# Two lengths in a planner's table, set to what the trace shows: transposing transfers and output products

## The chip, the cores and the metric

The kernel runs on one core of a Trainium2 chip. The metric is the device time of one execution in microseconds (us). It is given as the median of three runs; a profile is one further execution, with a time of its own.

## The reference

One hybrid encoder layer is applied to two sequences with the same weights: 1024 rows (prompt) and 4096 rows (sample), each row 1024 wide, all in float32.

```python
h = rms_norm(x, norm_g)
proj = h @ w_in                                   # 1024 -> 2816 columns
q, k, v, g_attn, u_conv, g_conv = split(proj)
attn = windowed_gqa(q, k, v, sink)                # 8 heads x 64, 128-row blocks, keys of 3 blocks
val, gate = split(u_conv)
c = depthwise_conv31(val * sigmoid(gate)) + dw_b  # 512 channels, 31 taps
conv = silu(layer_norm(c, ln_g, ln_b))
mix = concat(attn * silu(g_attn), conv * silu(g_conv))
y = rms_norm(x + mix @ w_out, final_g)
```

## The kernel before, in words

Rows are worked on in groups of 512 (two of the prompt, eight of the sample), and a group in four blocks of 128. Float32 products are made out of halves: a high and a low part, three products for each pair. The program has two stages, each recorded as a list of operations and then put in order by a planner.

**Stage A** (to about 896 us) makes the attention. `prep_x` normalizes a block of rows and splits it into high and low float16 parts (tile `xt`), and `dma_t` moves them, transposed, to the tile `x16` (`x` in the trace). `group_proj` makes keys, values, queries and gates from it with `inproj` (L347: 24 matmuls a tile, 128 weights columns by 512 rows). `attention` does one block: for each of two halves of the heads, four score products (L492, L493) into one of three PSUM tiles `s`; VectorE adds the distance penalty and takes the maximum (L496); ScalarE takes exponentials (L505) and normalizes (L512), VectorE makes the low part (L513), in one of three tiles `pe`; and `dma_t` moves `pe` transposed to a tile `pT`. When both halves have landed, TensorE makes the block's output `o` (L528, 18 matmuls, 12 at the ends of a sequence), VectorE and ScalarE multiply by the gate and split (L535, L536, L537), and the result goes to device memory (`md`). At its end the stage also makes the conv inputs of the first group: four tiles `h` (L638, L639) and four gates (L645), from the same `x16`.

**Stage B** makes the convolution, the output product and the final norm. For each group: load the next group's `x16` back (`x<-xd`), make its `h` tiles and gates (288 matmuls of L347), run 31 taps of the convolution over this group's four channel tiles on VectorE (L701, L703, tiles `acc`), turn `acc` on TensorE (L714) for the layer norm, turn it back (L750), and for each block make the output product from the stored attention part `ma` and the conv part `mc` (`out_mm`, L769, 24 matmuls each), add the residual (L800), and norm it on GpSimd (L803 and the lines 257 to 266, L813) before the store (`y`).

**The order.** `Plan.flush` is a list scheduler that runs when the kernel is built. Each operation is recorded with an engine and a cost in ns. The planner keeps a time for each engine and one for the transfers, picks whichever operation can start first (the earliest recorded one among equals), and emits them in order of planned start. Each engine, and the one queue of SyncE (SP) that issues all transfers, then works strictly in that order on the chip. The planner adds 1000 ns ahead of a transfer, `nbytes / 295` (transposing, `dma_t`) or `nbytes / 360` (plain, `dma`), one after the other, and 1600 ns behind. A transposing transfer of an attention half has 2048 x 384 = 786,432 bytes, of 2048 x 256 at the ends of a sequence; one of `xt` has 524,288. The cost of a pair of output matmuls in `out_mm` is 432 ns. Of VectorE's work the planner counts a tap (`c_dve(512, 1)`) as 663 ns.

```python
if o.eng == "SP":
    self.free["SP"] = s + 60.0
    self.dma = max(self.dma, s + 1000.0) + o.cost
    o.end = self.dma + 1600.0
```

Of the kernel before, what the change touches and what calls it, by code (L numbers as in the profile page):

```python
# [197 lines left out]
def hymba_kernel(ctx, tc, x_p, x_s, w_in, norm_g, sink, dw_w, vecs, w_out, final_g, dist, y_p, y_s):  # L198
    nc = tc.nc
    V, S, T, GP = nc.vector, nc.scalar, nc.tensor, nc.gpsimd  # L200
    PSUM = bass.MemoryType.PSUM
    pl = Plan(tc)
# [23 lines left out]
        pl.op("SP", nbytes / 360.0, lambda: nc.sync.dma_start(dst(), src()), r=r, w=w)  # L226

    def dma_t(dst, src, nbytes, r, w):
        pl.op("SP", nbytes / 295.0, lambda: nc.sync.dma_start(dst(), src(), transpose=True), r=r, w=w)

    ident = cst.tile([P, P], F32, name="ident")
    make_identity(nc, ident)
# [140 lines left out]
    def split_x(x16, b, xb, xt, rs, rv):  # L373
        pl.op("ACT", c_act(1024, 1), lambda: S.activation(xt.t[:, 0], xb.t, AF.Copy, scale=rv()), [xb, rs], [(xt, 0)])
        pl.op("DVE", c_dve(1024, 1), lambda: V.scalar_tensor_tensor(xt.t[:, 1], xb.t, rv(), xt.t[:, 0], ALU.mult, ALU.subtract), [xb, rs, (xt, 0)], [(xt, 1)])
        dma_t(lambda: x16.t[:, :, :, b * P : (b + 1) * P].rearrange("p a k t -> p (a k) t"), lambda: xt.t.rearrange("p a c -> p (a c)"), 524288, [xt], [(x16, b)])
# [88 lines left out]
    def attention(gi, qb, cur, prev):  # L465
# [11 lines left out]
        for kv in range(2):  # L477
            def one(kv=kv):
# [32 lines left out]
                for hh in range(4):  # L511
                    pl.op("ACT", c_act(n, 1), lambda hh=hh: S.activation(p16(hh, 0), sc_(hh), AF.Copy, scale=rc.t[:, hh : hh + 1]), [rc, (pe, hh + 2)], [(pe, hh)])  # L512
                    pl.op("DVE", c_dve(n, 1), lambda hh=hh: V.scalar_tensor_tensor(p16(hh, 1), sc_(hh), rc.t[:, hh : hh + 1], p16(hh, 0), ALU.mult, ALU.subtract), [rc, (pe, hh + 2)], [(pe, hh)])  # L513
                nk = len(kbs)
                dma_t(lambda: pT.t[:, : 8 * nk, :], lambda: flat().bitcast(F16)[:, : 8 * n], 2048 * n, [(pe, hh) for hh in range(4)], [pT])
                pTs.append(pT)
            one()
# [151 lines left out]
    wo = Buf(None, None, pb.tile([P, KD, 2, D], F32R, name="wo"))  # L669
# [94 lines left out]
    def out_mm(po, m, k0):  # L764
        for k in range(k0, k0 + 4):
            for a, b in ((0, 0), (0, 1), (1, 0)):
                def mm(k=k, a=a, b=b):
                    for hf in range(2):
                        T.matmul(  # L769
                            po[hf].t, m.t[:, a, k - k0, :], wo.t[:, k, b, hf * 512 : (hf + 1) * 512],  # L770
                            start=(k == 0 and a == 0 and b == 0), stop=(k == KD - 1 and a == 1),
                        )
                pl.op("PE", 432, mm, [(m, a) if k0 else m, (wo, k)], po)

    def out_first(gi, qb):
        si, g, n_g = groups[gi]
        ab = g * NB + qb
        src = seqs[si][0]
        tail = gi == NG - 1 and qb % 2 == 1
        xb = spare(qb, [P, D], F32) if tail and qb > 0 else pl.buf(pxA, [P, D], F32, "xb", 2)  # L780
        dma(lambda: xb.t, lambda: src[ab * P : (ab + 1) * P, :], 524288, [], [xb])
        ma = spare(0, [P, 2, 4, P], F32R) if tail else pl.buf(pb, [P, 2, 4, P], F32R, "ma", 1)
        md = mscr[si, ab]
        dma(lambda: ma.t.rearrange("p a j t -> p (a j t)").bitcast(F32), lambda: md.t, 524288, [md], [ma])
        po = [pl.buf(psq, [P, 512], F32, "mm", 4) for _ in range(2)]
        out_mm(po, ma, 0)
        return xb, po

    def out_second(gi, qb, xb, po, mc, eng="POOL"):
        en = GP if eng == "POOL" else V  # L790
        si, g, n_g = groups[gi]
        ab = g * NB + qb
        dst = seqs[si][1]
        out_mm(po, mc, 4)
        ms, v, rs = small(smB, 2, "ms2", 2), small(smB, 1, "v2", 2), small(smB, 1, "r2", 2)
        for hf in range(2):
            def half(hf=hf):
                xs = lambda: xb.t[:, hf * 512 : (hf + 1) * 512]
                sq = spare(4, [P, 512], F16) if gi == NG - 1 else po[hf]
                pl.op("DVE", c_dve(512), lambda: V.tensor_tensor(xs(), xs(), po[hf].t, ALU.add), [po[hf], (xb, hf)], [(xb, hf)])  # L800
                pl.op("ACT", c_act(512) + 100, lambda: S.activation(sq.t, xs(), AF.Square, scale=1.0 / math.sqrt(D), accum_out=ms.t[:, hf : hf + 1]), [(xb, hf)], [sq, (ms, hf)])  # L801
            half()
        pl.op(eng, 650 if en is GP else 140, lambda: en.tensor_scalar(v.t, ms.t[:, 0:1], ms.t[:, 1:2], EPS, ALU.add, ALU.add), [ms], [v])  # L803
        rsqrt(smB, rs, v, "o", eng)
        if en is V:
            for hf in range(2):
                def last(c=slice(hf * 512, (hf + 1) * 512), hf=hf):
                    pl.op("DVE", c_dve(512, 1), lambda: V.scalar_tensor_tensor(xb.t[:, c], xb.t[:, c], rs.t, fg.t[:, c], ALU.mult, ALU.mult), [(xb, hf), rs, fg], [(xb, hf)])
                    dma(lambda: dst[ab * P : (ab + 1) * P, c], lambda: xb.t[:, c], 262144, [(xb, hf)], [])
                last()  # L810
            return
        pl.op("ACT", c_act(1024, 1), lambda: S.activation(xb.t, xb.t, AF.Copy, scale=rs.t), [xb, rs], [xb])  # L812
        pl.op("POOL", 2400, lambda: GP.tensor_tensor(xb.t, xb.t, fg.t, ALU.mult), [xb, fg], [xb])  # L813
        dma(lambda: dst[ab * P : (ab + 1) * P, :], lambda: xb.t, 524288, [xb], [])

    curs[0]["gates"] = True
    for gi in range(NG):
# [16 lines left out]
        for b0, nb in chunks:  # L834
# [6 lines left out]
            for i in range(nb):  # L841
                xb, po = out_first(gi, b0 + i)
# [56 lines left out]
```

## Time and profile before

| | |
|---|---|
| median of three runs | 2024.65 us (2024.41 to 2028.73) |
| the profiled execution | 2031.13 us, its span 2029.3 us |
| busy: TensorE / VectorE / ScalarE / GpSimd | 92% / 89% / 45% / 33% of the span |
| mean granted TensorE clock | 0.983 of full speed |

The profile was taken in an execution 6.5 us above the median, and 1.8 us of its time lie outside the span. Times inside the trace are counted from the start of the span.

### The profile page before, as it was taken

The numbers are of one execution on the slowest core, as the hardware profiler recorded it, in microseconds if no ns is written. First come the engines' busy times: TensorE is split into PE (matmuls) and PEld (weight loads), VectorE is DVE, ScalarE is ACT, GpSimd is POOL, SyncE is SP. The second block draws the span as 40 slices with busy tenths as digits, with TensorE's granted clock in tenths as the row PEclk, the third lists the DMA queues.
The fourth block names the chain that finished last, engine by engine and source line by source line (L and its number), as shares of the span: only waits on it lengthen the run. The fifth ranks groups of instructions, "written<-read, shape, count | busy, mean of one in ns | idle before, by whom it ended". The sixth has DMA issues, their size and how long they took to land.

```text
span 2029.3 us, 26112 instructions
## 1 busy us (share of the span) xinstructions
PE 1874.0 (92%) x8953; PEld 1033.5 (51%) x8953; DVE 1809.5 (89%) x3779; ACT 904.5 (45%) x1962; POOL 670.8 (33%) x908
## 2 busy tenths in 40 slices
PE   2999999899999999989999899999999989999997
PEld 1444444444444444434647456474745647475675
DVE  6787988888978887879999899999989999898997
ACT  3576787787787876730303222220312212131332
POOL 3412233233321310000434627063461806143264
PEclk9999999999999999999999999999999999999999
DMA  7575979899989999772212211121221203123031
GB/s 243 148 174 131 241 186 230 192 197 225 223 192 242 221 300 272 149 238 84 94 42 94 83 68 68 52 95 42 94 73 59 89 21 123 42 94 104 25 122 73
DMA packets 367526, 276.18 MB, mean 136 GB/s; under 512 B 328736, under 2 KB 328864, under 8 KB 363808
## 3 DMA queue, kind: packets, MB, share of 16 engines
q1 hardware_dynamic: 367392, 274.51, 50.1%
q8 instruction: 70, 1.15, 0.2%
q14 instruction: 64, 0.52, 0.1%
HBM read 115.09 MB, written 77.59 MB: 95 GB/s over the span
## 4 chain that ended last, share of the span: by engine, by line
DVE 40%; PE 31%; DMA 10%; ACT 9%; POOL 6%; issue 3%; SPq 0%; DVEq 0%; ACTq 0%; POOLq 0%
DVE acc L703 23%; PE mm L347 16%; PE mm L769 10%; DMA pT<-pe 7%; DVE pe L496 3%; ACT pe L512 2%; ACT pe L505 2%; PE o L528 2%; DVE pe L513 2%; POOL rs_oa L264 1%; DVE xb L800 1%; DVE wA L703 1%; POOL xb L813 1%; POOL v L803 1%; DVE h L639 1%
## 5 line engine op out<-in xcount | busy, mean ns | idle before, releaser
L347 PE MATMUL mm<-x,wA 128*128 128x512 f16 x4800 | 1086.0, 382 | 14.7 <-DMA x<-xd 7.8
L703 DVE SCALAR_TENSOR_TENSOR acc<-h,taps,acc 128x512 f32<-128x512 f32 (+2 forms) x1380 | 867.7, 688 | 1.4
L347 PEld LDWEIGHTS <-wA 128*128 128x128 f16 x4800 | 468.5, 98 | 564.0 <-issue 29.5
L769 PE MATMUL mm<-wo,mc 128*128 128x512 f32 x960 | 236.5, 402 | 6.7 <-ACT mc L760 5.3
L769 PE MATMUL mm<-wo,ma 128*128 128x512 f32 x888 | 217.4, 400 | 7.5 <-DMA ma<-md 7.3
L496 DVE CUSTOM_DVE_ANT_0 pe<-s,dist_sb,sink_sb 128x384 f32<-128x384 f32 (+1 forms) x320 | 200.2, 658 | 21.3 <-DMA pT<-pe 11.5
L513 DVE SCALAR_TENSOR_TENSOR pe<-pe,rc 128x384 f16<-128x384 f32 (+1 forms) x320 | 190.2, 629 | 30.5 <-ACT pe L512 29.2
L803 POOL TENSOR_SCALAR v<-ms 128x1 f32<-128x1 f32 x38 | 46.9, 1233 | 509.7 <-ACT mm L801 498.9
L505 ACT ACTIVATE pe<-pe,nm 128x384 f32<-128x384 f32 (+1 forms) x320 | 188.9, 591 | 47.1 <-DVE nm L501 46.4
L769 PEld LDWEIGHTS mm<-wo,mc 128*128 128x128 f32 x960 | 180.3, 190 | 50.0 <-ACT mc L760 6.1
L512 ACT ACTIVATE pe<-pe,rc 128x384 f16<-128x384 f32 (+1 forms) x320 | 176.8, 593 | 37.1 <-DVE rc L509 21.9
L769 PEld LDWEIGHTS mm<-wo,ma 128*128 128x128 f32 x888 | 167.7, 189 | 49.1 <-issue 7.5
L812 ACT ACTIVATE xb<-xb,r 128x1024 f32<-128x1024 f32 x37 | 42.6, 1151 | 236.7 <-POOL r L266 236.7
L813 POOL TENSOR_TENSOR xb<-xb,fg 128x1024 f32<-128x1024 f32 x37 | 119.8, 3239 | 52.7 <-ACT xb L812 51.4
L638 ACT ACTIVATE h<-mm,ucolh 128x512 f32<-128x512 f32 x40 | 27.4, 685 | 218.6 <-PE mm L347 218.6
L492 PE MATMUL s<-kst,qst 128*128 128x384 f16 (+1 forms) x320 | 102.7, 323 | 19.6 <-DVE m L496 17.7
L347 PE MATMUL mm<-x,xt 128*128 128x512 f16 x480 | 112.4, 393 | 0.0
L528 PE MATMUL o<-pT,vst 128*64 128x512 f16 x696 | 93.6, 392 | 19.0 <-DMA pT<-pe 18.9
L757 ACT ACTIVATE xn<-c,vec_sb 128x128 f32<-128x128 f32 x160 | 60.4, 457 | 112.3 <-PE c L750 101.6
L493 PE MATMUL s<-kst,qst 128*128 128x384 f16 (+1 forms) x320 | 102.5, 322 | 0.0
L741 ACT ACTIVATE xn<-c,nmr,lrs 128x512 f32<-128x512 f32 x40 | 31.5, 788 | 113.5 <-DVE nmr L735 113.5
L264 POOL TENSOR_SCALAR rs_oa<-rs_oy,v 128x1 f32<-128x1 f32 x76 | 78.9, 1039 | 7.9
(163 smaller groups left out, 1904.9 us busy)
## 6 DMA issues: line engine op xcount, KB each, us to landing
xb<-x_s SPq DMA_DIRECT2D x62, 512.0 KB, 4.4
xd<-x SPq DMA_DIRECT2D x10, 2048.0 KB, 7.3
md<-mx SPq DMA_DIRECT2D x40, 512.0 KB, 3.3
x<-xd SPq DMA_DIRECT2D x10, 2048.0 KB, 7.8
ma<-md SPq DMA_DIRECT2D x37, 512.0 KB, 3.3
y_s<-xb SPq DMA_DIRECT2D x29, 512.0 KB, 2.6
wo<-od SPq DMA_DIRECT2D x8, 1024.0 KB, 16.4
xb<-x_p SPq DMA_DIRECT2D x14, 512.0 KB, 4.2
```

Of the source, the lines that this page charges most:

```text
L264: pl.op(eng, cost + 80, lambda: en.tensor_scalar(a.t, view(cur), view(cur), v.t, ALU.mult, ALU.mult), [cur, v], [a])
L347: T.matmul(ps.t, w16.t[:, a, k, :], x16.t[:, b, k, :], start=(k == 0 and i == 0), stop=(k == KD - 1 and i == 2))
L492: T.matmul(sv(), q, kst.t[:, 2 * kv, kc0 : kc0 + n], start=True, stop=False)
L493: T.matmul(sv(), q, kst.t[:, 2 * kv + 1, kc0 : kc0 + n], start=False, stop=True)
L496: pl.op("DVE", 198 + n / 0.96, lambda: V.tensor_tensor_reduce(sc_(hh), sv(), dist_b.t[:, kv, d0 : d0 + n], gcol[:, hh : hh + 1], sink_sb[: ...
L505: pl.op("ACT", 280 + 0.834 * n, lambda hh=hh: S.activation(sc_(hh), sc_(hh), AF.Exp, bias=nm.t[:, hh : hh + 1], accum_out=den.t[:, hh : hh ...
L512: pl.op("ACT", c_act(n, 1), lambda hh=hh: S.activation(p16(hh, 0), sc_(hh), AF.Copy, scale=rc.t[:, hh : hh + 1]), [rc, (pe, hh + 2)], [(pe ...
L513: pl.op("DVE", c_dve(n, 1), lambda hh=hh: V.scalar_tensor_tensor(p16(hh, 1), sc_(hh), rc.t[:, hh : hh + 1], p16(hh, 0), ALU.mult, ALU.subt ...
L528: T.matmul(o.t[r], vst.t[:, vb % NB, lo, kv, :], mov, start=(i == 0 and m == 0), stop=(i == nk - 1 and m == 2))
L703: pl.op("DVE", c_dve(n, 1), lambda: V.scalar_tensor_tensor(a.t[:, :n], src(), w, a.t[:, :n], ALU.mult, ALU.add), hr + [a], [a])
L769: T.matmul(po[hf].t, m.t[:, a, k - k0, :], wo.t[:, k, b, hf * 512 : (hf + 1) * 512], start=(k == 0 and a == 0 and b == 0), stop=(k == KD - ...
L813: pl.op("POOL", 2400, lambda: GP.tensor_tensor(xb.t, xb.t, fg.t, ALU.mult), [xb, fg], [xb])
```

## The change

Two numbers of the table that the planner reads are replaced. The bytes of a transposing transfer are divided by 177 in place of 295, so that one of 786,432 bytes counts 4.44 us in place of 2.67 us, and one of 524,288 bytes 2.96 us in place of 1.78 us. A pair of output matmuls counts 466 ns in place of 432 ns. What is computed, and the set of instructions but for reloads of ScalarE's function table, stay the same; their order is made anew on every engine.

```diff
     def dma_t(dst, src, nbytes, r, w):
-        pl.op("SP", nbytes / 295.0, lambda: nc.sync.dma_start(dst(), src(), transpose=True), r=r, w=w)
+        pl.op("SP", nbytes / 177.0, lambda: nc.sync.dma_start(dst(), src(), transpose=True), r=r, w=w)
...
-                pl.op("PE", 432, mm, [(m, a) if k0 else m, (wo, k)], po)
+                pl.op("PE", 466, mm, [(m, a) if k0 else m, (wo, k)], po)
```

Three places show the new order at the passage from stage A to stage B. First SP's queue, before: `pT` and `pe` are the two halves of the last attention block, `md` its stored result and that of the block ahead of it, `ma`, `xb` and `x_4947` the first loads of stage B.

```order
L229 DMA_TRANSPOSE pT_9387<-pe_9207 128x16x128
L226 DMA md_30_164<-mx_9430 128x1024
L229 DMA_TRANSPOSE pT_9459<-pe_9350 128x16x128
L226 DMA md_31_165<-mx_9503 128x1024
L226 DMA ma_9570<-md_0_98 128x1024
L226 DMA xb_9572<-x_p 128x1024
L226 DMA x_4947_9583<-xd_97 128x8192
```

The same place of SP's queue now; the two transfers of the last block are `pT_9482` and `pT_9521`.

```order
L229 DMA_TRANSPOSE pT_9414<-pe_9242 128x24x128
L226 DMA x_4947_9567<-xd_97 128x8192
L229 DMA_TRANSPOSE pT_9482<-pe_9323 128x16x128
L229 DMA_TRANSPOSE pT_9521<-pe_9425 128x16x128
L226 DMA md_30_164<-mx_9519 128x1024
L226 DMA xb_9571<-x_p 128x1024
L226 DMA md_31_165<-mx_9539 128x1024
L226 DMA ma_9573<-md_0_98 128x1024
```

The load of the second group's `x` has moved from behind everything that the last attention block issues to ahead of both its transposing transfers.

On VectorE, before, at the end of the last block (L513 is the low part of its second half, L535 and L537 its gate and split) and the start of the taps of stage B (L701, L703):

```order
L513 SCALAR_TENSOR_TENSOR pe_9350<-pe_9350,rc_9416 128x256 x2
L537 TENSOR_TENSOR mx_9430<-mx_9430 128x512
L513 SCALAR_TENSOR_TENSOR pe_9350<-pe_9350,rc_9416 128x256 x2
L535 TENSOR_TENSOR mx_9503<-o_9487,sg_8468 128x512
L537 TENSOR_TENSOR mx_9503<-mx_9503 128x512
L701 TENSOR_SCALAR acc_5031_9564<-h_170,taps,vec_sb 128x384
L701 TENSOR_SCALAR acc_5031_9568<-h_170,taps,vec_sb 128x384
```

The same place on VectorE now; `o_9526` is the last block's output.

```order
L513 SCALAR_TENSOR_TENSOR pe_9425<-pe_9425,rc_9488 128x256 x4
L535 TENSOR_TENSOR mx_9519<-o_9492,sg_8388 128x512
L537 TENSOR_TENSOR mx_9519<-mx_9519 128x512
L535 TENSOR_TENSOR mx_9539<-o_9526,sg_8388 128x512
L537 TENSOR_TENSOR mx_9539<-mx_9539 128x512
L701 TENSOR_SCALAR acc_5031_9565<-h_170,taps,vec_sb 128x384
L701 TENSOR_SCALAR acc_5031_9569<-h_170,taps,vec_sb 128x384
```

The taps stand behind the last block's L535 and L537 in both; now the results of the last two blocks come right behind each other there.

On ScalarE, before, the first gate (L645) and its table load stand behind every exponential (L505) and every L512:

```order
L505 ACTIVATE pe_9350,den_9392<-pe_9350,nm_9382 128x256 x3
L512 ACTIVATE pe_9350<-pe_9350,rc_9416 128x256 x2
L536 ACTIVATE mx_9430<-mx_9430 128x512
L512 ACTIVATE pe_9350<-pe_9350,rc_9416 128x256 x2
L645 ACT_TABLE_LOAD
L645 ACTIVATE x_4839_9448<-mm_9362,ucol 128x512
```

And now, for the last block (`mm_9382` and `mm_9439` are the third and the fourth gate's products):

```order
L645 ACT_TABLE_LOAD
L645 ACTIVATE x_4839_9329<-mm_9382,ucol 128x512
L512 ACTIVATE pe_9323<-pe_9323,rc_9431 128x256 x2
L503 ACT_TABLE_LOAD
L503 ACTIVATE es_9458<-dl_9451 128x4
L505 ACTIVATE pe_9425,den_9460<-pe_9425,nm_9449 128x256 x2
L512 ACTIVATE pe_9425<-pe_9425,rc_9488 128x256 x2
L645 ACT_TABLE_LOAD
L645 ACTIVATE x_4839_9329<-mm_9439,ucol 128x512
L536 ACTIVATE mx_9519<-mx_9519 128x512
```

The gates have moved in among the last blocks' exponentials, and the program has five table loads there in place of one. On TensorE the 24 matmuls of the fourth gate (the last that read the first group's `x`) stood behind all of the attention before; now the last two blocks' L528 (18 and 12 matmuls) stand behind them. In the middle of stage A each block's L528 stands further behind its last score product. In stage B the turn of `acc` (L714) stands 18 matmuls of L347 further ahead in the third and in the fourth of the ten groups; from there on TensorE's order is the same but for the last group, and VectorE has one tap or more added between a block's L761 and the next L759.

## Rows read from the trace of the kernel before

**Rows 1.** The page's head and part 1: span, busy time of each engine.

```profile
span 2029.3 us, 26112 instructions
PE 1874.0 (92%) x8953; PEld 1033.5 (51%) x8953; DVE 1809.5 (89%) x3779; ACT 904.5 (45%) x1962; POOL 670.8 (33%) x908
```

**Rows 2.** Busy time by stretch, us: PE, PEld, DVE, ACT, POOL; clock, DMA share, GB/s.

```profile
50.00:896.00 846.00, 793.84 (x4073) 371.45 (x4071) 698.54 (x1806) 626.27 (x1422) 206.51 (x436) 0.99 0.87 206
896.00:977.00 81.00, 72.26 (x332) 35.25 (x332) 80.83 (x160) 9.35 (x16) 0.85 (x1) 0.96 0.42 166
977.00:1431.00 454.00, 432.60 (x1967) 260.21 (x1968) 442.58 (x807) 100.91 (x201) 199.62 (x180) 0.98 0.19 66
```

**Rows 3.** Waits of PE, then of DVE, 0 to 905: us, times, longest us.

```profile
PE o L528 <- DMA pT<-pe: 18.9, 16, 2.5
PE s L492 <- DVE m L496: 17.7, 21, 2.1
...
DVE mx L535 <- PE o L528: 27.1, 15, 7.7
...
DVE pe L496 <- DMA pT<-pe: 11.5, 12, 2.7
```

**Rows 4.** SP's timeline, three attention halves issued together: start, us.

```profile
821.11 14.52 SPq L229 DMA_TRANSPOSE pT<-pe  x3
...
880.09 2.77 SPq L229 DMA_TRANSPOSE pT<-pe  x1
```

**Rows 5.** PE's timeline around the passage: start, us, what, idle before it.

```profile
870.75 0.27 PE L492 MATMUL s<-kst,qst 128*128 128x256 f16 x1
...
886.19 1.49 PE L528 MATMUL o<-pT,vst 128*64 128x512 f16 x12
887.60 7.94 PE L347 MATMUL mm<-x,xt 128*128 128x512 f16 x36
903.39 53.90 PE L347 MATMUL mm<-x,wA 128*128 128x512 f16 x240 [7.84 <-DMA x<-xd]
...
976.33 0.66 PE L750 MATMUL c<-ident,xn 128*128 128x128 f32 x4 [1.33 <-ACT xn L741]
```

**Rows 6.** DVE's timeline, then ACT's, around the passage.

```profile
879.15 0.87 DVE L513 SCALAR_TENSOR_TENSOR pe<-pe,rc 128x256 f16<-128x256 f32 x2
887.74 0.69 DVE L535 TENSOR_TENSOR mx<-o,sg 128x512 f32<-128x512 f32 x1 [7.71 <-PE o L528]
...
889.78 0.86 DVE L701 TENSOR_SCALAR acc<-h,taps,vec_sb 128x384 f32<-128x384 f32 x2
...
879.32 1.28 ACT L645 ACT_TABLE_LOAD   x1
880.62 0.69 ACT L645 ACTIVATE x<-mm,ucol 128x512 f32<-128x512 f32 x1
```

**Rows 7.** PE's timeline, first output product of three later groups.

```profile
1553.08 5.95 PE L769 MATMUL mm<-wo,ma 128*128 128x512 f32 x24
...
1672.82 5.95 PE L769 MATMUL mm<-wo,ma 128*128 128x512 f32 x24
...
1785.88 5.96 PE L769 MATMUL mm<-wo,ma 128*128 128x512 f32 x24
```

**Rows 8.** Waits of DVE, 905 to 2030; then groups of instructions by line.

```profile
DVE h L639 <- ACT h L638: 14.5, 3, 6.3
DVE xn L759 <- ACT xn L757: 12.4, 16, 2.3
...
L703 DVE SCALAR_TENSOR_TENSOR acc<-h,taps,acc 128x512 f32<-128x512 f32 x900 | 659.9, 789 | 1.4
```

**Rows 9.** POOL's timeline, one final multiplication; DVE's, who waited behind it.

```profile
1471.58 11.58 POOL L813 TENSOR_TENSOR xb<-xb,fg 128x1024 f32<-128x1024 f32 x1 [1.27 <-ACT xb L812]
1488.39 2.34 POOL L813 TENSOR_TENSOR xb<-xb,fg 128x1024 f32<-128x1024 f32 x1 [1.26 <-ACT xb L812]
...
1489.43 1.28 DVE L800 TENSOR_TENSOR xb<-xb,mm 128x512 f32<-128x512 f32 x2 [8.48 <-DMA xb<-x_s]
```

## The prediction

> **What bounds the kernel now.** I read the shares first, then the busy time by stretch, then the waits of the two busiest engines, and last the timeline where stage A passes into stage B. TensorE (PE) is busy for 1874.0 of 2029.3 us and VectorE (DVE) for 1809.5 [rows 1]; neither share says which of them to look at, so the stretches do. From 50 to 896 us, stage A, PE is busy for 793.84 of 846 us and DVE for 698.54: PE sets the pace, and 52 us of it are idle [rows 2]. From 896 to 977 us DVE is busy for 80.83 of 81 us, and from 977 to 1431 us for 442.58 of 454, while PE has 9 and 21 us free: there DVE sets the pace [rows 2]. So a us that DVE's taps start later at the passage comes out a us later at 1431.
>
> What PE waits for in stage A is the first thing that the change addresses. Sixteen of the forty blocks' outputs (L528) wait for the transposed tile `pT`, 18.9 us in all and 2.5 us at most; score products wait 17.7 us for DVE's maximum, 21 times [rows 3]. DVE in turn waits 27.1 us for those outputs and 11.5 us for transposing transfers that still read a `pe` tile [rows 3]. Both say that transposes come later than the order assumes.
>
> **The change part by part.** *The transposing transfers in stage A.* Three issued together hold SP's queue for 14.52 us, 4.84 each [rows 4]. For 786,432 bytes that is 162 bytes a ns, so 177 (4.44 us) is much nearer than 295 (2.67 us). The new order plans each landing 1.78 us later, and both halves queue behind each other, so L528 moves back. Counted over the forty blocks, the matmuls between a block's last score product and its first L528, at the trace's pace (53.90 us for 240 of L347, the others in proportion to their rows), grow from 20.0 to 22.8 us on average. The added 2.8 us are more than the longest of the sixteen waits, so most should go. They were 18.9 us; the added distance is uneven, so I take 14. DVE's 38.6 us behind outputs and transposes shrink as well, and with them some of the 17.7 us that scores wait for DVE; I take 3. Together 17 us less before the passage. Bounds: 0, if PE then waits for DVE in the same places, and 36.6, if both kinds of wait go entirely.
>
> [...]
>
> *The passage.* Call T the moment when PE has finished the last matmul on the first group's `x`; only then can SP load the second group's. Before, T is 887.60 + 7.94 = 895.54 [rows 5]. In the new order the last two blocks' 18 and 12 output matmuls come behind T. Twelve take 1.4 us to the next start (886.19 to 887.60), so thirty take 3.5 us [rows 5], and T comes 3.5 us earlier, besides the 17.
>
> The taps (L701, L703) stand on DVE behind L537 of the last block. Before, they start at 889.78, which is T - 5.8 [rows 6]. In the new order the last block's last score products are followed by the fourth gate's 24 matmuls (5.2 us), so they lie at about T - 5.5. From the last score products to the end of the last L513 took 870.75 to 880.02, 9.3 us [rows 5, 6]; that gives T + 3.8. On the way ScalarE (ACT) now reloads its table twice, 1.28 us each, and does a gate of 0.69 us that can't begin before T [rows 6]; part of this runs while ACT would have waited for DVE, so I add 1.7 of 3.25: T + 5.5. The transpose and the first L528 took from 880.09 to 886.19, 6.1 us [rows 4, 5]: T + 11.6. The last outputs, L535, L536 and L537 follow: 886.19 to 889.78 is 3.6 us, so T + 15.2 [rows 5, 6]. The taps start at T + 15 in place of T - 5.8, 20.8 us later against T. Bounds are T + 11.5 (both reloads hidden, nothing else late) and T + 18 (all of the 3.25 on the path, and 1.3 for the load of 2 MB that stands ahead in the queue). That load itself hides: it takes 7.84 us [rows 5], which the last block's chain covers.
>
> What is queued behind it: the taps, 69 us of them in the first chunk, then everything of the layer norm, and L750 on PE, where PE had only 1.33 us of waiting [rows 5]. So PE waits there for DVE, and no cover is left. The first chunk thus moves by 20.8 - 3.5 - 17 = +0.3 us. Bounds: with the ends of both terms, 17.3 - 3.5 - 36.6 = -22.8 and 23.8 - 3.5 - 0 = +20.3.
>
> *The output products in stage B.* At 466 ns a pair the plan agrees with PE: 24 matmuls and a turn follow each other there at the trace's pace, and DVE's order fits it. In the order before, DVE is sent to L759 and to the next group's L639 too early: it waits 12.4 us in 16 places for L759 and 14.5 us in three for L639 [rows 8]. The groups that begin with the output products at 1553.08 and 1672.82 take 119.74 and 113.06 us, the second being nearly all PE work [rows 7]; the difference of 6.7 us is what a better order can give back in one group, and I take about one such group in all, 6 us. Against it stands that in two groups L714 comes 18 matmuls earlier, 3.9 us of filler each that PE then has behind L714 and not ahead of it, up to 7.8 us if PE waits there. I take 0.3 for it, as DVE has the pace up to 1431 us [rows 2], and PE's waiting ahead of L714 costs nothing as long as that is so. Stage B together: -5.7 us, bounds -20 (most of the 26.9 us of DVE's two waits) and +7.8. The changed places in the last group (a few output matmuls ahead of or behind L714) lie on a PE that is full there; I count them at nothing, at most 1 us.
>
> *The first 50 us.* The first L347 now stands behind two small matmuls in place of ahead of them: within 1 us either way, counted at nothing.
>
> **The sum.** +0.3 - 5.7 = -5.4 us, on 2031.13 us of the profiled execution (2029.3 of span and 1.8 outside) 2025.7. That execution is 6.5 us above the median, so for the median I predict 2024.65 - 5.4 = 2019.2 us.
>
> **The rivals.** *Slower, by the passage.* The attention's tail is what decides if stage A gives back little: PE's 18.9 us behind transposes turn into waits for DVE, which is itself busy for 83% of stage A. With 4 us saved in place of 17 and stage B at -2, the sum is 20.8 - 3.5 - 4 - 2 = +11 us, 2036. It decides from the point at which less than about 8 us go in stage A. For it: the tail's 20.8 us are certain in kind, the saving is spread over sixteen small waits. Against it: DVE's own waits are caused by the same transposes. Chance 0.24, between 2029 and 2045.
>
> *No change.* The saving and the tail cancel, and stage B is held by DVE alone (97% busy up to 1431), so that PE's waits only move from L750 to L714: 2024.65 within 4 us (0.2%, about what a measurement of this kernel can tell from no change). For it: a tap takes 789 ns in the mean where the plan counts 663 [rows 8], an error that remains and that the old, too low cost of PE partly balanced. Chance 0.27.
>
> *Slower, by GpSimd.* The multiplication L813 takes 2.34 us where DVE leaves it room and 11.58 us beside a run of taps; in the second case the store, the next load of `xb` and then DVE's L800 come late, 8.48 us [rows 9]. An order that fills DVE's gaps with taps can make one more such event: 8.5 us on top of the forecast, +3.1 us, two of them +11.6, so 2028 to 2036. [...] Chance 0.07 beyond 2029.
>
> *The transposes are short.* [...] The 4.84 us speak against it: 0.02.
>
> **How the numbers follow.** My forecast, with its own range of 2004 to 2020.5, has 0.40; no change 0.27; the three slower cases 0.33. The range for 8 in 10 leaves out about one tenth on each side: below, a saving near the bound of stage A together with a good stage B (2024.65 - 19); above, the upper end of the rival by the passage. That makes 2006 to 2037.
>
> **What would show it.** Right: PE's waits for `pT` in stage A fall from 18.9 to about 5 us, those for DVE's maximum to below 17; T comes at about 875 (895.54 - 20.5); L701 starts some 15 us behind T, near 890; ACT has five table loads near the passage; PE waits 10 us or more ahead of the first L714 or L750 where it waited 1.33; DVE's waits at L639 and L759 fall. Wrong: T near 890 (stage A gave nothing), taps that start behind 895, or DVE's busy share after 1431 that falls because GpSimd's L813 is blocked more often.

## The result, and the profile after

The changed kernel takes 2059.66 us (median of 4 runs, 2052.99 to 2065.54) beside 2024.53 us before: ratio 1.0151, 95% interval 1.0127 to 1.0175. It is slower by 35 us between the medians and by 26 to 35 us in the interval, where 5 us faster was forecast. The profiled execution takes 2061.77 us, its span 2060.0 us, 30.7 us more than before [rows 1].

The page's head and part 1 of the changed kernel:

```profile
span 2060.0 us, 26135 instructions
...
PE 1876.8 (91%) x8953; PEld 1031.4 (50%) x8953; DVE 1790.8 (87%) x3779; ACT 911.9 (44%) x1966; POOL 662.8 (32%) x908
```

PE is as busy as before and DVE 19 us less: the two have no more work, they wait longer. Where, the busy time by stretch of the changed kernel shows (columns as in [rows 2], whose stretches the first three are):

```profile
50.00:896.00 846.00, 794.36 (x4104) 368.35 (x4103) 690.83 (x1792) 633.08 (x1427) 201.14 (x435) 0.98 0.86 207
896.00:977.00 81.00, 66.31 (x299) 32.73 (x297) 81.00 (x162) 7.18 (x12) 1.31 (x1) 0.92 0.38 154
977.00:1431.00 454.00, 426.31 (x1923) 256.18 (x1924) 423.16 (x782) 98.15 (x194) 200.85 (x180) 0.97 0.18 66
```

From 977 to 1431 DVE, which set the pace there, is busy for 423.16 us in place of 442.58 [rows 2]. SP's timeline of the changed kernel, at the loads of the groups' `x`, gives the growth group by group:

```profile
876.24 0.32 SPq L226 DMA_DIRECT2D x<-xd  x1
...
1080.08 0.32 SPq L226 DMA_DIRECT2D x<-xd  x1
...
1328.08 0.32 SPq L226 DMA_DIRECT2D x<-xd  x1
1451.53 0.32 SPq L226 DMA_DIRECT2D x<-xd  x1
1575.29 0.32 SPq L226 DMA_DIRECT2D x<-xd  x1
1690.05 0.32 SPq L226 DMA_DIRECT2D x<-xd  x1
1803.11 0.32 SPq L226 DMA_DIRECT2D x<-xd  x1
```

Before, the last six stood at 1075.16, 1313.91, 1431.42, 1553.47, 1673.20 and 1786.26. So the changed kernel is behind by 4.9, 14.2, 20.1, 21.8, 16.9 and 16.9 us, and by 30.7 at the end. Nearly all is lost in stage B. The changed kernel's waits in stage B, of DVE and then of PE (us, times, longest us):

```profile
DVE xb L800 <- DMA xb<-x_s: 51.5, 7, 10.2
DVE h L639 <- ACT h L638: 13.5, 3, 10.0
DVE xb L800 <- DMA xb<-x_p: 8.8, 1, 8.8
...
DVE xn L759 <- ACT xn L757: 5.6, 7, 1.3
```

```profile
PE c L750 <- ACT xn L741: 29.0, 10, 7.6
PE mm L769 <- DMA ma<-md: 21.3, 4, 9.3
PE c L714 <- DVE acc L703: 20.3, 7, 12.7
```

PE's three were 23.6, 7.3 and 8.1 us before; 12.7 of the 20.3 us for `acc` lie at the passage. DVE waits 60.3 us in eight places for `xb`, the block's rows of `x` that L800 adds. Before it was 12.6 us in two places, of which [rows 9] show one:

```profile
DVE xb L800 <- DMA xb<-x_s: 8.5, 1, 8.5
...
DVE xb L800 <- DMA xb<-x_p: 4.1, 1, 4.1
```

How one such wait comes about, the timeline of the changed kernel shows:

```profile
1612.30 1.27 DVE L800 TENSOR_TENSOR xb<-xb,mm 128x512 f32<-128x512 f32 x2
1613.49 7.37 DVE L703 SCALAR_TENSOR_TENSOR acc<-h,taps,acc 128x512 f32<-128x512 f32 x11
...
1614.88 8.20 POOL L813 TENSOR_TENSOR xb<-xb,fg 128x1024 f32<-128x1024 f32 x1 [1.27 <-ACT xb L812]
...
1623.11 0.34 SPq L226 DMA_DIRECT2D y_s<-xb  x1
...
1626.09 0.33 SPq L226 DMA_DIRECT2D xb<-x_s  x1
...
1629.37 1.28 DVE L800 TENSOR_TENSOR xb<-xb,mm 128x512 f32<-128x512 f32 x2 [8.51 <-DMA xb<-x_s]
```

L813 comes 1.4 us into a run of eleven taps and ends only 2.2 us after the last of them: 8.20 us, where 2.34 do when it has room [rows 9]. Store, load and L800 follow, and DVE, whose own taps held L813 up, waits 8.51 us for it. The same place of the group in the kernel before:

```profile
1592.32 14.82 DVE L703 SCALAR_TENSOR_TENSOR acc<-h,taps,acc 128x512 f32<-128x512 f32 x19
1593.34 2.64 POOL L813 TENSOR_TENSOR xb<-xb,fg 128x1024 f32<-128x1024 f32 x1 [1.27 <-ACT xb L812]
...
1596.01 0.34 SPq L226 DMA_DIRECT2D y_s<-xb  x1
...
1598.80 0.33 SPq L226 DMA_DIRECT2D xb<-x_s  x1
...
1607.07 1.27 DVE L800 TENSOR_TENSOR xb<-xb,mm 128x512 f32<-128x512 f32 x2
```

There L813 gets in after one tap (0.74 us), it is the next tap that is held up (2.88 us), and the next L800 does not wait. Of 38 L813, 11 take over 4 us in the changed kernel and 6 before.

Two things go beyond L813's length. In these rows DVE has 19 taps between the two L800 in the old order and 11 in the new, so the new order leaves the chain of store, load and L800 less room: with an L813 of 2.64 us in place of 8.20 the wait of 8.51 us would be 5.56 us shorter by my estimate, and 3 us of it would stay. And GpSimd's work isn't held up longer in sum: it is busy for 662.8 us in the changed kernel and for 670.8 before, L813 for 30 us more, the norm's small steps for 34 us less. What has grown is the number of its delays that DVE and PE stand behind.

### The profile page after: what moved, and what is told of

Read it like the earlier page. It is cut to its first block, busy times and chain, and to the rows that moved or that the text cites. A ratio compares the mean times of both kernels' runs of the same rounds, so it can differ in the third digit from the quotient of the medians.

```text
span 2060.0 us, 26135 instructions
## 1 busy us (share of the span) xinstructions
PE 1876.8 (91%) x8953; PEld 1031.4 (50%) x8953; DVE 1790.8 (87%) x3779; ACT 911.9 (44%) x1966; POOL 662.8 (32%) x908
## 4 chain that ended last, share of the span: by engine, by line
DVE 40%; PE 32%; ACT 12%; POOL 9%; issue 4%; DMA 3%; SPq 0%; DVEq 0%; POOLq 0%; ACTq 0%
DVE acc L703 22%; PE mm L347 16%; PE mm L769 12%; ACT pe L505 4%; DVE pe L496 3%; DVE pe L513 3%; POOL xb L813 3%; ACT pe L512 2%; PE o L528 2%; POOL rs_oa L264 1%; DVE qst L458 1%; DVE h L639 1%; DVE xb L800 1%; POOL rs_xa L264 1%; PE s L492 1%
## 5 line engine op out<-in xcount | busy, mean ns | idle before, releaser
L347 PE MATMUL mm<-x,wA 128*128 128x512 f16 x4800 | 1090.0, 382 | 23.3 <-ACT mm L801 10.0
L703 DVE SCALAR_TENSOR_TENSOR acc<-h,taps,acc 128x512 f32<-128x512 f32 (+2 forms) x1380 | 851.1, 676 | 1.8
L347 PEld LDWEIGHTS <-wA 128*128 128x128 f16 x4800 | 470.7, 98 | 574.1 <-issue 42.1
L769 PE MATMUL mm<-wo,ma 128*128 128x512 f32 x888 | 221.8, 405 | 21.3 <-DMA ma<-md 21.3
L513 DVE SCALAR_TENSOR_TENSOR pe<-pe,rc 128x384 f16<-128x384 f32 (+1 forms) x320 | 192.3, 638 | 31.2 <-ACT pe L512 30.4
L505 ACT ACTIVATE pe<-pe,nm 128x384 f32<-128x384 f32 (+1 forms) x320 | 188.9, 591 | 55.1 <-DVE nm L501 54.9
L803 POOL TENSOR_SCALAR v<-ms 128x1 f32<-128x1 f32 x38 | 33.4, 878 | 541.5 <-ACT mm L801 526.7
L512 ACT ACTIVATE pe<-pe,rc 128x384 f16<-128x384 f32 (+1 forms) x320 | 176.2, 594 | 36.5 <-DVE rc L509 18.9
L813 POOL TENSOR_TENSOR xb<-xb,fg 128x1024 f32<-128x1024 f32 x37 | 150.0, 4054 | 50.8 <-ACT xb L812 50.7
L812 ACT ACTIVATE xb<-xb,r 128x1024 f32<-128x1024 f32 x37 | 42.5, 1149 | 237.1 <-POOL r L266 237.1
L347 PE MATMUL mm<-x,xt 128*128 128x512 f16 x480 | 114.4, 398 | 0.0
L800 DVE TENSOR_TENSOR xb<-xb,mm 128x512 f32<-128x512 f32 x76 | 48.6, 679 | 67.5 <-DMA xb<-x_s 51.5
L741 ACT ACTIVATE xn<-c,nmr,lrs 128x512 f32<-128x512 f32 x40 | 31.4, 786 | 124.0 <-DVE nmr L735 122.2
L528 PE MATMUL o<-pT,vst 128*64 128x512 f16 x696 | 84.0, 384 | 0.5 <-DMA pT<-pe 0.5
## 6 DMA issues: line engine op xcount, KB each, us to landing
wo<-od SPq DMA_DIRECT2D x8, 1024.0 KB, 15.2
```

Of the source, the lines that this page charges most:

```text
L347: T.matmul(ps.t, w16.t[:, a, k, :], x16.t[:, b, k, :], start=(k == 0 and i == 0), stop=(k == KD - 1 and i == 2))
L505: pl.op("ACT", 280 + 0.834 * n, lambda hh=hh: S.activation(sc_(hh), sc_(hh), AF.Exp, bias=nm.t[:, hh : hh + 1], accum_out=den.t[:, hh : hh ...
L528: T.matmul(o.t[r], vst.t[:, vb % NB, lo, kv, :], mov, start=(i == 0 and m == 0), stop=(i == nk - 1 and m == 2))
L703: pl.op("DVE", c_dve(n, 1), lambda: V.scalar_tensor_tensor(a.t[:, :n], src(), w, a.t[:, :n], ALU.mult, ALU.add), hr + [a], [a])
L769: T.matmul(po[hf].t, m.t[:, a, k - k0, :], wo.t[:, k, b, hf * 512 : (hf + 1) * 512], start=(k == 0 and a == 0 and b == 0), stop=(k == KD - ...
```

## The experiments

Medians of the kernel before moved between 2024.5 and 2030.4 us from one chip job to the next, so each run is compared with those of its own job.

**Which number.** One number at a time: `dma_t` at 177 with products at 432, and the reverse.

> Only the transposing transfers are counted longer (177), output products stay at 432. Theory 1 (the loss comes from stage B, where the new order of the output products lets GpSimd's final multiplication L813 be blocked behind runs of taps, so that the store, the next xb and the next ma come late): stage B keeps the old order from the fourth group on, so only the 3.4 us by which the taps start later in the changed kernel (893.22 against 889.78) and the first groups are left: 2020 to 2030 us, DVE waits no more than 20 us at L800 for xb. Rival (the passage with its five table loads and the late taps cost it): 2045 us or more.

> Only the output products are counted longer (466), transposing transfers stay at 295. Theory 1: stage A and the passage are as before (taps start at 889.8), stage B takes the loss of the changed kernel, 31 - 3 = 27 us: 2043 to 2058 us, with 40 us or more of DVE waiting at L800 for xb and 15 us or more of PE waiting for ma. Rival (the passage): within 6 us of the kernel before, 2019 to 2031.

Measured: transposes alone 2027.32 us beside 2027.25 (1.0008, 0.9990 to 1.0026); products alone 2059.51 (1.0163, 1.0139 to 1.0188). The second number carries all of the loss. DVE's waits at L800 with it alone:

```profile
DVE xb L800 <- DMA xb<-x_s: 42.8, 7, 8.6
...
DVE xb L800 <- DMA xb<-x_p: 8.6, 1, 8.6
```

**Is it the long multiplication?** L813 on 64 columns, all orders as they were:

```diff
-        pl.op("POOL", 2400, lambda: GP.tensor_tensor(xb.t, xb.t, fg.t, ALU.mult), ...
+        pl.op("POOL", 2400, lambda: GP.tensor_tensor(xb.t[:, 0:64], xb.t[:, 0:64], fg.t[:, 0:64], ALU.mult), ...
```

> [...] Theory 1: DVE's waits at L800 for xb fall from 60 us to below 15 and PE's for ma from 21 to below 5; 2005 to 2033 us. Rival (the new order itself costs, by the distances between PE's and DVE's work, whatever GpSimd does): 2045 us or more, PE's waits at L714 and L750 stay near 49 us.

> The kernel before with the same shortened L813, as the control: taps that stood behind L813 are no longer stretched either, so it should gain too. Theory 1: it comes within 8 us of the changed kernel with the same edit, as what told the two orders apart is gone: 2000 to 2022 us. Rival: it stays 20 us or more below it.

Measured: 2007.96 us for the changed order, 1969.66 for the old one. Both gain over 50 us, but 38 us between them stay. So the length of the multiplication alone is not the cause, and theory 1 falls in that form.

**Is it SP's queue?** In the steady groups the fourth load of `ma` stands behind a store in the new order and ahead of it in the old. A step behind the sort exchanges the two, other engines untouched:

```diff
+            if not a.w and load(b) == "ma" and n >= 3:
+                out.remove(a)
+                out.insert(out.index(b) + 1, a)
```

> The changed kernel with SP's queue alone edited: from each group's fourth load of ma on, the load stands ahead of the store that stood before it (PE, DVE, ACT and GpSimd rows unchanged). Theory 2 (what the longer output products cost is one place of SP's queue: a load of ma behind a store that waits for GpSimd's L813): PE's waits for ma fall from 21.3 to below 8 us, and at least 18 of the 32 us come back, 2025 to 2042 us. Rival (the taps between VectorE's L800s are badly placed, whatever SP does): 2052 us or more.

> The kernel before with SP's queue alone edited the other way: in the three groups in which the fourth ma stands ahead of the second store it is put behind it, as it stands in the groups before them (117.5, 122.1 and 119.7 us there, 113.06 in the steady ones). Theory 2: the three groups take 116 to 120 us, the kernel 2035 to 2047. Rival (VectorE's order matters, the load is covered): within 5 us of the kernel before.

> The changed kernel with a third number in the table set to what the trace shows: L813 counts 4000 ns in place of 2400 (4054 is its mean in the profile). The planner then puts the fourth ma ahead of the second store by itself, and moves VectorE's rows too. Theory 2: 2025 to 2042 us. Rival: 2052 us or more.

> The changed kernel with SP's queue edited as in the first of these runs, and L813 on 64 of the 1024 columns (the gain left out for the others). The same shortening gave 2008.0 us for the changed kernel and 1969.7 for the one before. Theory 2: the 38 us between those two go for the most part, 1970 to 1985 us, no waits of PE for ma above 2 us. Rival: 2000 us or more.

Measured: 2060.31 us for the changed kernel with the exchange, though PE's waits for `ma` fell from 21.3 to 12.5 us, and 2030.24 beside 2030.36 for the reverse in the kernel before. Theory 2 falls from both sides. Counting L813 as 4000 ns gives 2052.47 (1.0118, 1.0096 to 1.0141), and the exchange with the shortened L813 2016.68: neither comes near. The last of these showed what had been overlooked. GpSimd's timeline there (its L817 is L803 of the other kernels, its lines 271 to 280 are the norm's small steps):

```profile
1560.12 7.11 POOL L817 TENSOR_SCALAR v<-ms 128x1 f32<-128x1 f32 x1 [63.88 <-ACT mm L815]
...
1579.47 0.30 POOL L817 TENSOR_SCALAR v<-ms 128x1 f32<-128x1 f32 x1 [0.92 <-ACT mm L815]
```

An instruction on one column takes 7.11 us beside a run of taps and 0.30 without. So the norm's small steps can be held up too, not only L813. In the changed kernel the longest of the eight waits, 10.2 us, comes behind two small steps of 6.4 us each (L803 at 1231.08 and L266 at 1246.46), with an L813 of 2.35 us.

**All of GpSimd's reads away.** The norm's eleven steps and L813 only write constants (512 columns, the last step one, L813 twice 1024), at the same planned costs and places:

```diff
-        pl.op(eng, cost, lambda: en.tensor_scalar(yi.t, v.t.bitcast(I32), ...
+            pl.op(eng, cost, lambda: GP.memset(junk.t[:, 0:512], 0.0), [v], [yi])
...
+        pl.op("POOL", 2400, lambda: [GP.memset(xb.t, 0.0) for _ in range(2)], [xb, fg], [xb])
```

> The changed kernel, rows of PE, VectorE, ScalarE and SP unchanged; GpSimd's final norm (L803, lines 257 to 266, L813) only writes constants, 512 or 1024 columns at a time and so about as long as planned, and reads nothing (the final norm is left out). Theory 3 (the loss comes from GpSimd's reads that wait out whole runs of VectorE's taps, at other moments in the two orders): this and the kernel before with the same edit lie within 8 us of each other, 1955 to 1995 us. Rival (the order of PE and VectorE costs by itself): the changed one is 20 us or more slower.

> The kernel before with the same edit (GpSimd's final norm writes constants and reads nothing; the final norm is left out), as the control. Theory 3: within 8 us of the changed kernel with that edit, 1955 to 1985 us. Rival: 20 us or more faster than it.

Measured: 1971.75 us (1969.56 to 1973.68) for the changed order and 1969.54 (1962.31 to 1973.45) for the old one. Of 35 us between the orders 2.2 are left, within the spread. The orders of PE, DVE, ACT and SP are those of the two kernels, and they cost nothing without GpSimd's reads: the loss needs these reads beside DVE's taps. It is not shown that every one of the 35 us is a read waiting out a run. In both runs PE is busy for all but 0.4 us of a steady group, so a new order with less room for DVE could also hide here. One such group of the changed order, then of the old one, columns as in [rows 2]:

```profile
1516.60:1627.69 111.09, 110.67 (x513) 67.46 (x512) 99.05 (x166) 26.82 (x53) 28.94 (x52) 1.00 0.21 76
```

```profile
1508.30:1619.40 111.10, 110.68 (x513) 67.42 (x512) 107.83 (x179) 26.93 (x53) 28.81 (x52) 1.00 0.22 76
```

**The passage.** The gates' Silu also depends on the last block's `pe`, with 177 and 432:

```diff
-..., [ps, (ucol_b, c)], [(sgc, (i, j))])
+..., [ps, (ucol_b, c)] + pl.last, [(sgc, (i, j))])
```

> Transposing transfers at 177, output products at 432, and the four gates of the first group made to depend on the last block's exponentials, so that ScalarE keeps one table load at the passage. By the prediction's passage step (two reloads and a gate in the last block's chain, the load of x ahead of its transposes) the taps start earlier by 5 to 12 us than the 893.8 of the run with 177 alone, and the kernel takes 2012 to 2022 us. Rival (the last block is paced by its own chain on VectorE and the transposing transfers, whose late start is not due to the reloads): taps after 890, 2023 us or more.

Measured: one table load, taps at 887.63 us, 6.2 earlier than with 177 alone, and 2022.98 us beside 2029.8 (0.9972, 0.9957 to 0.9988). The time lies 1 us outside the range that was expected. The late taps come in part from where the gates stand; the reloads and the gates moved together, so the reloads alone are not priced.

**The moment of a read.** Two, or four, writes of one column behind each L803, of which the planner knows nothing:

```diff
+            first = [0] * 2
...
+        pl.op(eng, cost, lambda: [GP.memset(yi.t, 0) for _ in first] + [en.tensor_scalar(yi.t, ...
```

> The changed kernel, every other engine's rows unchanged; behind each L803 GpSimd writes two constants of one column (about 0.1 us each) before the norm goes on, of which the planner knows nothing. Theory 3, in the form that the moment within a tap at which a GpSimd read arrives decides if it waits for one tap or for the run: the long L813 of the changed kernel (arrivals 65 to 91 ns behind a tap's start) arrive about 200 ns later in a tap, most of them shrink below 3 us, and the time falls by 10 us or more, below 2048, although work was added. Rival (what counts is where the runs stand, not tens of ns): 2052 to 2068 us.

> The kernel before with four such writes behind each L803, about 0.4 us. Theory 3 in that form: the arrivals that pass now (L813 276 to 360 ns behind a tap's start in the last groups) move to the other end of a tap or just behind the next start, some then wait out a run, and the kernel takes 2036 us or more. Rival: within 6 us of the kernel before.

Measured: the changed kernel with two 2064.67 us (2046.75 to 2067.43), no gain. The kernel before with four 2053.14 beside 2028.98 (1.0101, 1.0078 to 1.0124): 0.4 us a block (0.10 for one write) on an engine that is a third busy cost 24 us. Its timeline (L804 is L800, L817 is L813):

```profile
1844.76 1.27 DVE L804 TENSOR_TENSOR xb<-xb,mm 128x512 f32<-128x512 f32 x2
1845.96 8.03 DVE L707 SCALAR_TENSOR_TENSOR acc<-h,taps,acc 128x512 f32<-128x512 f32 x12
...
1847.28 8.91 POOL L817 TENSOR_TENSOR xb<-xb,fg 128x1024 f32<-128x1024 f32 x1 [1.27 <-ACT xb L816]
...
1862.30 1.29 DVE L804 TENSOR_TENSOR xb<-xb,mm 128x512 f32<-128x512 f32 x2 [8.31 <-DMA xb<-x_s]
```

L813 takes 8.9 us in one block of each of the last three steady groups, where the kernel before had 2.7. So in the old order, every other engine's order untouched, other moments of GpSimd's reads, with 0.4 us a block of added work, cost two thirds of what the change does. That the two writes gained nothing is a miss. L813 over 4 us fell from 11 to 7 and DVE's waits for `xb` from 60.3 to 42.3 us, but PE's waits for `ma` rose from 21.3 to 31.4. Four of the seven still come 79 to 97 ns behind the start of a tap, as would follow if a small read that has waited ties the rest of the chain to a tap's end again. In the changed kernel 81 of the 93 small steps that take over 1 us between 896 and 1960 us end 48 to 92 ns behind a tap's end; whether that is what places L813 no run tested.

**Versions with a complete output.** L812 and L813 of every block become two DVE instructions as L808, or the whole norm goes to DVE as in the last two blocks:

```diff
+                pl.op("DVE", c_dve(512, 1), lambda: V.scalar_tensor_tensor(xb.t[:, c], xb.t[:, c], rs.t, fg.t[:, c], ALU.mult, ALU.mult), ...
```

> The kernel before with ScalarE's L812 and GpSimd's L813 replaced by two VectorE instructions of 0.71 us each, in the form that L808 has in the last blocks, for every block. VectorE gets 37 x 1.42 = 53 us more work and loses the 2.2 us by which a tap is held up behind most of the 37 L813 (some 30 x 2.2 = 66 us). Theory 3: the norm chain loses the longest of its waits, 1990 to 2018 us. Rival (VectorE's work alone counts): within 8 us of the kernel before.

> The changed kernel (177 and 466) with the last multiplication of the final norm on VectorE; the small GpSimd reads of the norm stay. The kernel before with that edit took 2012.6 us. If L813 alone carried the loss of the change: 2005 to 2020 us. If the small reads carry it too: 2030 us or more.

> The kernel before with the whole final norm of every block on VectorE, in the form that the last two blocks have, so GpSimd reads nothing in stage B beside the taps, and the output is complete. Some 11 small instructions of about 0.2 us and two of 0.71 us a block come to VectorE, 37 x 3.6 = 133 us less what fills gaps, and 60 us of held-up taps go. If VectorE's load decides: 2040 us or more. If the waits behind GpSimd decide: 1990 to 2020 us.

> The changed kernel with the same edit. Theory 3: with GpSimd's reads gone the two numbers of the change no longer cost anything: within 8 us of the kernel before with the same edit. Rival (the order costs by itself): 20 us or more slower than it.

> Transposing transfers at 177, output products at 432, the four gates behind the last exponentials, and the last multiplication of the final norm on VectorE in two instructions of 0.71 us. If the two gains add up (17 us and 7 us, as each was measured against the kernel before): 1998 to 2010 us. Rival (what the earlier taps gain is lost again behind GpSimd's small reads, at other moments): 2012 to 2025 us.

Measured: the multiplication on DVE gives 2012.55 us on the kernel before (0.9921, 0.9898 to 0.9944), and 2031.51 on the changed one (1.0017, 1.0002 to 1.0033). So 19 us between the costs stay without L813. That the small reads that are left carry them is not shown: DVE waits 41.8 us for the last of them with the new costs and 27.7 with the old, but both orders are made anew. With the whole norm on DVE the kernel before takes 2045.95 and the changed one 2026.12: the sign turns, so an order made anew can be worth 20 us without GpSimd's reads. These 20 us lie behind the last load of `x` (1763.95 and 1763.41 us), where PE waits for the last group's taps (tiles `wA`). PE's wait there with the old costs, then its waits with the new ones:

```profile
PE c L714 <- DVE wA L703: 27.2, 2, 27.0
```

```profile
PE c L714 <- DVE acc L703: 13.0, 2, 12.7
PE c L714 <- DVE wA L703: 9.9, 2, 9.7
```

The combined version takes 2011.95 us beside 2029.76 (0.9924, 0.9898 to 0.9949): the two gains don't add up, but it and the simpler one beat both kernels.

## Why the prediction was wrong

**Stage A and the passage: right in the sum, in part by luck.** PE's waits for `pT` fell from 18.9 to 0.5 us (about 5 forecast). T is 870.87 + 5.34 = 876.21 (875 forecast), and L701 starts at 893.22, T + 17.0 (T + 15.2 forecast). The first taps moved by 3.4 us (0.3 forecast), and PE waits 12.7 us ahead of the first L714 (10 or more forecast). PE's and DVE's waits up to 905 us in the changed kernel:

```profile
PE s L492 <- DVE m L496: 29.0, 29, 2.9
...
PE mm L347 <- DMA x<-xt: 7.0, 1, 7.0
...
PE o L528 <- DMA pT<-pe: 0.5, 2, 0.3
```

```profile
DVE den L507 <- ACT pe L505: 36.9, 29, 2.9
```

But the way there was another. The 3 us expected of PE's waits for DVE's maximum did not come; they rose from 17.7 to 29.0 [rows 3]. The attention gained and lost: the thirtieth block's L535 starts at 710.58 in place of 731.19, the thirty-fourth's at 800.58 in place of 800.50. Between lie the 7.0 us for `x` and 14.4 of the 36.9 us that DVE waits for exponentials. So the last block's last score products come at 870.65, as before (870.75) [rows 5]: what stage A saved was PE's other work. That T came so near the forecast is in part luck, as one of the two terms moved the other way. That the attention lost its gain just there is read off the trace; no run tested it. PE's own timeline, ACT's and DVE's, at the passage:

```profile
870.65 0.27 PE L492 MATMUL s<-kst,qst 128*128 128x256 f16 x1 [0.62 <-DVE m L496]
...
870.87 5.34 PE L347 MATMUL mm<-x,xt 128*128 128x512 f16 x24
```

```profile
869.56 1.28 ACT L645 ACT_TABLE_LOAD   x1
...
872.35 1.28 ACT L503 ACT_TABLE_LOAD   x1
...
878.24 1.28 ACT L645 ACT_TABLE_LOAD   x1
```

```profile
893.22 0.86 DVE L701 TENSOR_SCALAR acc<-h,taps,vec_sb 128x384 f32<-128x384 f32 x2
```

Five table loads, as forecast. The run with 177 alone bears the sum out: 1.0008, no change.

**Stage B: the step that failed** is "Stage B together: -5.7 us, bounds -20 and +7.8". It weighed only PE against DVE, and left what GpSimd does to both out of its sum and out of its bounds. What it weighed did move as meant: the wait at L759 shrank from 12.4 to 5.6 us (that at L639 hardly, 14.5 to 13.5), and the group priced at 119.74 us takes 114.76 now, from the load of `x` at 1575.29 to the next, so most of the 6 us came there. The number 466 is not the error either: in the changed kernel 24 products that start at 1826.18 us have 5.61 us to PE's next instruction, 467 ns a pair. But the waits behind GpSimd were only a rival, at "one more such event" of 8.5 us, two at most, with 0.07. There were six more, 47.7 us of waiting, and the products alone cost 32 us where 5.7 were to be gained. The prediction's own sign of being wrong came: from 1431 to 1786 us DVE is busy for 322.18 us, where it was 331.52. The mechanism was named, with its rows; mis-sized was how often it strikes. In the changed kernel a wait of 8.5 to 8.6 us at L800 comes once in each of four groups in a row (1385.78, 1509.54, 1629.37 and 1744.26 us): an unlucky meeting repeats with the loop, and a bound of one or two events was no bound.

**The other rivals.** "Slower, by the passage" gave 2036 and did not happen. Short transposes are out: counted longer, they let stage A lose its waits for `pT` (18.9 to 0.5 us).

## What to carry to other kernels

A planner's table that is made truer in one number can make the kernel slower, if another engine's times depend on whom it meets; look for the engine whose same instruction has two durations in the trace (2.34 and 11.58 us here) and ask what the new order makes it meet, in every repeat of the loop. Before costing such a change by its distances, take the meeting away in an experiment on both orders: here 35 us shrank to 2. What paid here was to take the one long read off that engine (2012.55 us beside 2029.8 in the old order); taking all of them off to DVE cost 17 us there (2045.95 beside 2028.98), so price the work that the other engine gets.

## What the runs showed of the hardware

Beside back-to-back taps of 128x512 (in both traces one most often starts 0.663 us after the other), GpSimd's L813 waits for one tap (2.64 us at 1593.34 in the kernel before) or for the rest of the run (8.20 us at 1614.88 in the changed one), and which of the two goes with where in a tap it arrives. For the ten runs with L813 in full I subtracted the start of the tap in progress from the start of each L813 with at least four more taps behind it, between 1040 and 1960 us: 185 cases, 55 of them over 4 us. Of 44 that came 50 to 150 ns behind a tap's start 39 were long, of 129 at 150 to 600 ns 9, of 9 at 600 ns or later 7, of 3 below 50 ns none. The limits of these classes are read off the same cases, and of the two runs that moved the moment one bears them out and one does not. The row of the changed kernel at 1614.88 came 0.07 us behind the third tap, that of the kernel before at 1593.34 0.36 behind the second. Why the moment decides stays open, and so does which row of the new order moves it.

One wait of PE cost 1.6 us more than itself. Behind the 4.59 us for `ma` the 24 products take 7.38 us, the next 24 take 5.76, in PE's timeline of the changed kernel:

```profile
1842.56 7.38 PE L769 MATMUL mm<-wo,ma 128*128 128x512 f32 x24 [4.59 <-DMA ma<-md]
1849.78 5.76 PE L769 MATMUL mm<-wo,mc 128*128 128x512 f32 x24
```

The granted clock there, by stretch (columns as in [rows 2]), is 0.53 for the first 3.64 us and 1.00 behind:

```profile
1842.56:1846.20 3.64, 3.64 (x9) 2.87 (x10) 1.78 (x3) 2.21 (x4) 2.09 (x5) 0.53 0.31 108
1846.20:1849.90 3.70, 3.70 (x17) 2.97 (x17) 3.70 (x5) 0.28 (x2) 3.41 (x4) 1.00 0.36 142
```

GpSimd's reads also cost the kernel before: without them it takes 1969.54 us beside 2029.8, 60 us less. Nearly all of it is L813: shortened to 64 columns, with the small reads left as they were, it gave 1969.66 us beside 2027.25.
